# Reordering the down products of both feed-forwards and moving x1's division by its rms behind W_in's products

## The chip, the cores and the metric

The kernel runs on one core of a Trainium2 chip. The metric is device time in microseconds (us) of one execution; lower is better. TensorE (PE) does the matmuls, VectorE (DVE), ScalarE (ACT) and GpSimd (POOL) the elementwise work, SyncE (SP) issues most DMAs. Matmul results land in PSUM, everything else on the chip lies in SBUF.

## The reference

One layer of a streaming encoder in fp32, 1024 tokens of width 1024:

```
x1  = x  + 1/2 * SwiGLU_1(RMSNorm(x))          # 1024 -> 2*2816 -> 2816 -> 1024
h   = RMSNorm(x1)                              # x1 / rms(x1) * g_mix
q_A,k_A,v_A,q_B,k_B,v_B,gate_A,gate_B = h @ W_in
y   = sigmoid(gate_A)*(A(q_A,k_A,v_A) @ W_upA) + sigmoid(gate_B)*(B(q_B,k_B,v_B) @ W_upB)
x2  = x1 + y @ W_out
x3  = x2 + 1/2 * SwiGLU_2(RMSNorm(x2))
out = RMSNorm(x3)
```

A is chunked attention, B differential attention; both normalize q and k by head (an rms over 64 columns) before use. v and the gates are used as they come from W_in.

## The kernel before, in words

Every fp32 matmul is made of three: each operand is split into a rounded high part (a cast on ACT) and the remainder (a subtraction on DVE), and high*high, high*low and low*high are summed in PSUM (`mm3`, recorded at line 90). The split of a weight is lines 211 (ACT) and 215 (DVE), that of a stored hidden activation lines 785 (ACT) and 788 (DVE), that of the last hidden tiles 770 and 771, that of a transposed operand 448 (ACT) and 449 (DVE, reading PSUM).

**Down projection.** The 22 blocks of 128 hidden channels fall into two groups that are multiplied in the manner of Strassen and Winograd (`paired`: two groups of five pairs of blocks) and two plain blocks (`down`). A group has seven products, in the order of the tuple `PRODUCTS`. A product runs over five pairs and four row blocks c, 60 matmuls of 128x512, into four PSUM banks. `down_operand` makes the weight sums that products 3 to 6 need, on POOL (lines 352 to 358: T for products 5, 6 and 4, b12 for product 3). `quarter_sums` takes each of the four banks out of PSUM into the quarters c11, c12, c21, c22 of x or into the shared sums u2, a5, a7 (line 830). In the second group, `end`, the shared sums are added to the quarters on POOL: c22 += a5 after product 5; a5 += u2, c12 += a5 and a7 += u2 after product 6; c21 += a7 and c22 += a7, eight additions of 128x512, are kept in `later` and issued by `down` for its tiles t = 0 to 3. `residual` adds the saved first half of x to c11 on POOL in the first group.

**`down`** does for each row tile t of 128 rows and each half of 512 columns the two plain blocks: 6 matmuls into one bank, and line 916 on DVE adds it to x. Then it calls `done`, which is `after1` in the first feed-forward and `after2` in the second.

**`after1`** stores x1, norms it (`Norm`: Square with a running sum on ACT at line 475, the root on POOL at lines 455 and 456, x * 1/rms * gain on DVE at line 482), and `transpose_into_xT` turns the normed tile by eight PE transposes and splits it into xTh and xTl, the operand of W_in. **`after2`** norms x3 in the same way and stores the output.

**W_in** follows: for each group of 512 columns and each row tile 24 matmuls into a bank. q and k tiles are squared (ACT, 1136), summed by head (DVE, 1139), rooted (POOL, 455 and 456), scaled (DVE, 1145) and turned. v is split by 1196 (ACT) and 1197 (DVE), a gate copied by 1207 (ACT).

**What sets the order.** The program is written in the order of PE's work. Other work hangs on `pe.chain(keys, (delay, function), ...)`: a function is issued once PE's stream has gone on by that many ns, and `pe.settle(key)` issues what is still open on a key. So each engine's queue has a fixed order, and an instruction that waits holds up all behind it on its engine.

```
pe.chain((), (1000, store), (1300, norm.scale), (1600, lambda: norm.into_xT(t)))   # after1
pe.chain((), (1000, norm.stats), (2000, norm.scale), (1300, store))                # after2
```

Of the kernel before, what the change touches and what calls it, by code (L numbers as in the profile page):

```python
# [21 lines left out]
P = 128  # L22
# [29 lines left out]
assert PLAIN + 2 * sum(GROUPS) == NF  # L52
PRODUCTS = (1, 2, 5, 6, 4, 3, 7)

# [200 lines left out]
def kernel(ctx, tc, io, out):  # L255
# [17 lines left out]
    lam = cp.tile([P, 2], F32, name="lam")  # L273
    nlam = cp.tile([P, 1], F32, name="nlam")


# [49 lines left out]
    def ffn_weights(w_gu, w_down):  # L326
# [16 lines left out]
        def down_operand(p, top, bottom, ts, i):  # L343

            def piece():
                (b11, b12), (b21, b22) = [(w[:, :512], w[:, 512:]) for w in (weights.raw[top], weights.raw[bottom or top])]
                engine = nc.gpsimd
                if p == 5:  # L350
                    ts[i] = pools["T"][:, i] if i < 4 else pe.tile(pools["ffn"], [P, 512], F32, "sg", 3)
                    engine.tensor_tensor(ts[i], b12, b11, op=ALU.subtract)
                elif p == 6:
                    engine.tensor_tensor(ts[i], b22, ts[i], op=ALU.subtract)
                elif p == 4:
                    engine.tensor_tensor(ts[i], b21, ts[i], op=ALU.subtract)
                elif p == 3:
                    engine.tensor_tensor(b12, b22, b12, op=ALU.subtract)
                return {1: b11, 2: b21, 3: b22, 7: b12}.get(p, ts.get(i))

            if p == 1:
                return lambda: weights.raw[top][:, :512], top, [], 0
            return piece, top if p == 5 else bottom, {3: [bottom], 7: [top]}.get(p, []), p in (3, 4, 5, 6)

# [132 lines left out]
    def ffn(pool, base, x_d, begin, when, after, gain, beside):  # L497
# [234 lines left out]
        class Hidden:  # L732
# [27 lines left out]
            def load_last(self):  # L760

                while len(self.rooms) >= 2 and self.n_last < PLAIN:
                    f = self.n_last
                    raw = last_raw(f)
                    h, l = last[f] = [
                        pool.tile([P, S], F32R, name="hl", tag=self.rooms.popleft()) for _ in range(2)
                    ]
                    pe.chain(
# [3 lines left out]
                    )  # L772
                    self.n_last += 1

            def next(self):
# [29 lines left out]

        hidden, last, hs = Hidden(), {}, {}

# [14 lines left out]
        def quarter_sums(n, p, c, ps):  # L822
# [12 lines left out]
            if p == 1:  # L835
                now = [copy(u2, ps)] if first else [plus(c11, ps), plus(u2, ps)]
            elif p == 2:
                now = [plus(c11, ps, u2) if first else plus(c11, ps)]
            elif p == 6:
# [10 lines left out]
            elif end and p == 6:  # L850
                pe.chain(
                    (x[c], ("acc", c)), (900, plus(a5, u2, engine=nc.gpsimd)),
                    (LATE, plus(c12, a5, engine=nc.gpsimd)), (LATE, plus(a7, u2, engine=nc.gpsimd)),
                )
            elif end and p == 7:
                later[c] = (x[4 + c], ("acc", c)), (0, plus(c21, a7, engine=nc.gpsimd)), (LATE, plus(c22, a7, engine=nc.gpsimd))

        later = {}

        def paired():  # L860
# [10 lines left out]
            for n, g in enumerate(GROUPS):  # L871
                for p in PRODUCTS:
# [16 lines left out]
                    if n == 0 and p in (2, 5):  # L889
                        for t in range(4, NT) if p == 2 else range(4):  # L890
                            cols = slice(0 if t >= 4 else 512, D)
                            nc.sync.dma_start(x[t][:, cols], x_d[t * P : (t + 1) * P, cols])
                    if n == 0 and p in (4, 3, 7) or (n, p) == (1, 1):
                        residual((4, 3, 7, 1).index(p))
                    if (n, p) == (1, 3):
                        gain()
            nth = first + -(-j // 2)

        def down(fs, done):

            first = nth
            for t in range(NT):
                ts = slice(t * P, (t + 1) * P)
                for c in range(2):
# [13 lines left out]
                    pe.chain((ps, x[t]), (610, add))  # L918
                if t < 4:
                    pe.chain(*later[t])  # L920
                elif t == 4:
                    for c in range(4):
# [69 lines left out]
    def after1(t, xt):  # L992

        if t == 0:
            new_xT(0)
        elif t == 4:
            new_xT(1)
        norm = Norm(fp, xt, gm[0])

        def store():  # L1000
            pe.settle(xt)
            nc.sync.dma_start(x1_d[t * P : (t + 1) * P, :], xt)
            norm.stats()

        pe.chain((), (1000, store), (1300, norm.scale), (1600, lambda: norm.into_xT(t)))

# [81 lines left out]
    def project_all(cols, evac):  # L1088

        for col in cols:  # L1090
            first = base_in + 4 * (col // 512)
            for t in range(NT):
                ps = banks["fill"]() if "fill2" not in banks or t % 2 == 0 else banks["fill2"]()
                pe.settle(("xT", t))
                for k in range(NK):
# [32 lines left out]
    def qk_evac(n, t, ps):  # L1128
# [6 lines left out]
        def square():  # L1135
            nc.scalar.square(qn, ps)

# [3 lines left out]
        def root():  # L1141
            box["r"] = rstd_of(ap, ss, HD, 8, "rs8")

        def normed():
# [44 lines left out]
    def v_evac(n, t, ps):  # L1189
# [5 lines left out]
            (ps, stg),  # L1195
            (95, lambda: nc.scalar.copy(sv[:, :, 0], ps3)),
            (600, lambda: nc.vector.tensor_tensor(sv[:, :, 1], ps3, sv[:, :, 0].bitcast(F32), op=ALU.subtract)),
            (1390, lambda: nc.sync.dma_start(v_d[n][t], stg.bitcast(F32))),
        )

    def g_evac(n, t, ps):
# [4 lines left out]
            (ps, gs),  # L1206
            (150, lambda: nc.scalar.copy(gs, ps)),
            (700, lambda: nc.sync.dma_start(g_d[t, :, i, c * 512 : (c + 1) * 512], gs)),
# [525 lines left out]
    def after2(t, xt):  # L1734
        norm = Norm(fp, xt, gf[0])

        def store():
            nc.sync.dma_start(out[t * P : (t + 1) * P, :], norm.y)

        pe.chain((), (1000, norm.stats), (2000, norm.scale), (1300, store))  # L1740

# [41 lines left out]
```

## Time and profile before

| | |
|---|---|
| median of 3 runs | 2212.17 us (2210.03 to 2213.1) |
| the profiled execution | 2211.59 us |
| its span, first to last instruction | 2209.5 us |
| mean granted TensorE clock | 0.990 |
| PE busy | 2139.8 us (97%) |
| DVE, ACT, POOL busy | 1449.5 (66%), 851.0 (39%), 846.1 (38%) us |

The span is cut into 40 slices of 55.2 us in the page's second part; each digit there is a busy share in tenths. Places are given in us from the span's start. The first feed-forward's paired products end and its plain ones begin at 644.95, the second's at 2165.76. In the timeline a row of several instructions gives their common time; a matmul's own time (0.39) is longer than the step from one to the next, since they are pipelined. A number in square brackets at the end of a row is the idle time before it, and what ended it.

### The profile page before, as it was taken

How to read it: one execution, taken by the hardware profiler on the slowest of the kernel's cores; microseconds unless marked ns; L12 is line 12 of the kernel's file. 1: busy time of each engine (PE TensorE's matmuls, PEld its weight loads, DVE VectorE, ACT ScalarE, POOL GpSimd, SP SyncE). 2: the span in 40 equal slices, each digit the busy share in tenths (PEclk: the TensorE clock that was granted, in tenths of full speed). 3: DMA queues.
4: the chain of work that ended last, by engine and by line, in shares of the span. 5: the costliest groups of instructions: out<-in, count | busy, mean ns of one | idle time of the engine just before them, and what ended most of it. 6: DMA issues, size and time to landing. Idle time of an engine off the chain costs nothing. (4 is left out here: it accounts for less than half of the span.)

```text
span 2209.5 us, 27922 instructions
## 1 busy us (share of the span) xinstructions
PE 2139.8 (97%) x10112; PEld 1783.0 (81%) x10112; DVE 1449.5 (66%) x2021; ACT 851.0 (39%) x1483; POOL 846.1 (38%) x749
## 2 busy tenths in 40 slices
PE   7999999999998998999999999999999999999996
PEld 6788888888876887888888887788788888888885
DVE  7768666687985435775665662534766666668895
ACT  5323323244333224665555552313332332334431
POOL 3645544352762313552111110000554545426483
PEclk9999999999999999999999999999999999999998
DMA  4234333376342445756544439523132332365431
GB/s 158 77 94 135 101 115 101 123 258 202 115 150 90 132 159 170 196 150 193 169 137 136 153 115 268 193 77 118 54 103 90 105 103 91 114 231 210 152 117 77
DMA packets 267602, 305.66 MB, mean 138 GB/s; under 512 B 17456, under 2 KB 177480, under 8 KB 267464
## 3 DMA queue, kind: packets, MB, share of 16 engines
q1 hardware_dynamic: 267320, 303.35, 43.1%
q8 instruction: 80, 1.31, 0.2%
q14 instruction: 58, 0.48, 0.1%
q0 software_dynamic: 144, 0.52, 0.1%
HBM read 210.21 MB, written 94.40 MB: 138 GB/s over the span
## 5 line engine op out<-in xcount | busy, mean ns | idle before, releaser
L211 ACT CAST wh<-w 128x1024 fp32r<-128x1024 f32 (+1 forms) x228 | 201.1, 900 | 400.7 <-PE mm L90 147.8
L90 PE MATMUL fill<-wh,xTh 128*128 128x512 f32 x824 | 328.1, 405 | 0.0
L90 PE MATMUL fill<-wh,xTl 128*128 128x512 f32 x816 | 315.2, 393 | 0.0
L215 DVE TENSOR_TENSOR wl<-w,wh 128x1024 fp32r<-128x1024 f32 (+1 forms) x227 | 286.7, 1278 | 35.3 <-ACT wh L211 34.8
L90 PE MATMUL fill<-wl,xTh 128*128 128x512 f32 x752 | 296.6, 394 | 0.0
L90 PE MATMUL mm<-xTl,wh 128*128 128x512 f32 (+1 forms) x572 | 220.7, 386 | 2.4 <-DVE xTl L614 1.8
L90 PE MATMUL mm<-xTh,wh 128*128 128x512 f32 (+1 forms) x572 | 221.6, 387 | 0.2 <-ACT xTh L448 0.2
L90 PE MATMUL mm<-xTh,wl 128*128 128x512 f32 (+1 forms) x572 | 220.2, 385 | 0.0
L90 PE MATMUL mm<-S,wh 128*128 128x512 f32 x640 | 197.0, 389 | 0.0
L90 PEld LDWEIGHTS fill<-wh,xTl 128*128 128x128 f32 x816 | 154.0, 189 | 33.1
L90 PEld LDWEIGHTS fill<-wh,xTh 128*128 128x128 f32 x824 | 155.7, 189 | 27.2
L90 PEld LDWEIGHTS fill<-wl,xTh 128*128 128x128 f32 x752 | 142.7, 190 | 23.3
L455 POOL TENSOR_SCALAR rs<-ss 128x1 f32<-128x1 f32 (+1 forms) x64 | 13.1, 205 | 337.2 <-ACT xn L475 237.6
L90 PEld LDWEIGHTS mm<-S,wh 128*128 128x128 f32 x640 | 120.1, 188 | 24.9
L215 DVE TENSOR_TENSOR wl<-tw,wh 128x1024 fp32r<-128x1024 f32 x80 | 124.9, 1562 | 9.3 <-ACT wh L211 9.3
L90 PEld LDWEIGHTS mm<-xTl,wh 128*128 128x128 f32 x572 | 108.6, 190 | 24.5 <-DVE xTl L614 2.2
L90 PE MATMUL mm<-wh,xTh 128*128 128x512 f32 x376 | 126.7, 390 | 0.0
L90 PEld LDWEIGHTS mm<-xTh,wh 128*128 128x128 f32 x572 | 108.6, 190 | 21.7 <-ACT xTh L448 0.7
L90 PEld LDWEIGHTS mm<-xTh,wl 128*128 128x128 f32 x572 | 108.4, 190 | 21.4 <-POOL wl L215 0.2
L90 PE MATMUL mm<-S,wl 128*128 128x512 f32 x320 | 124.5, 389 | 0.0
L90 PE MATMUL mm<-wh,xTl 128*128 128x512 f32 x360 | 121.3, 389 | 0.0
L335 POOL TENSOR_TENSOR tw<-w,w 128x512 f32<-128x512 f32 x40 | 55.0, 1376 | 152.2 <-DVE wl L215 103.7
(254 smaller groups left out, 4851.8 us busy)
## 6 DMA issues: line engine op xcount, KB each, us to landing
w<-in_w_ffn_gu SPq DMA_DIRECT2D x88, 512.0 KB, 4.3
raw<-hq_d SPq DMA_DIRECT2D x70, 512.0 KB, 3.7
hq_d<-xn SPq DMA_DIRECT2D x98, 256.0 KB, 4.5
w<-in_w_ffn_down SPq DMA_DIRECT2D x44, 512.0 KB, 5.6
w<-in_w_in SPq DMA_DIRECT2D x40, 512.0 KB, 4.3
hq_d<-x SPq DMA_DIRECT2D x42, 256.0 KB, 4.3
x_d<-x SPq DMA_DIRECT2D x16, 512.0 KB, 3.2
uq<-qa_d SPq DMA_DIRECT2D x32, 256.0 KB, 4.5
```

The lines of the kernel that those rows point to most:

```text
L90: self.nc.tensor.matmul(ps, lhs, rhs, **flags)
L211: self.nc.scalar.copy(h, w)
L215: (lo_engine or self.nc.vector).tensor_tensor(l, w, h.bitcast(F32), op=ALU.subtract)
L335: nc.gpsimd.tensor_tensor(t[:, :512], u0, g0, op=ALU.subtract)
L455: nc.gpsimd.tensor_scalar(r, ss, 1.0 / n, EPS, op0=ALU.mult, op1=ALU.add)
```

## The change

1. `PRODUCTS` becomes (1, 2, 5, 6, 7, 4, 3). Product 7 makes b12 itself; products 4 and 3 come last and take T and the raw b22. POOL's a7 += u2, c21 += a7 and c22 += a7 of the second group hang on product 7, so `later` goes. In the first group ACT copies both u2 and c11 out of product 1. The calls of `residual` and `gain` move.
2. `after1` has no norm any more. POOL multiplies x1 by the gain (line 1011 of the changed kernel, 128x1024), into the place of hidden tiles that are no longer used; ACT's Square sums into a column of `ss_x1`; after the last tile POOL makes all eight `r_x1` = 1/rms. The product x1 * gain is turned, and W_in's results are multiplied by `r_x1` where they leave PSUM: in the scale of ACT's Square for q and k with one POOL multiplication more on the head roots (line 1160), in ACT's copies for v and gates, and in DVE's subtraction for v. The transposes are due 4300 ns of PE's stream behind the store rather than 1600 behind the scale.
3. `after2` takes its normed tile from four such places, and the scale is due 2600 ns behind the statistics rather than 2000.

```diff
-PRODUCTS = (1, 2, 5, 6, 4, 3, 7)
+PRODUCTS = (1, 2, 5, 6, 7, 4, 3)
...
-                elif p == 3:
+                elif p == 7:
                     engine.tensor_tensor(b12, b22, b12, op=ALU.subtract)
                 return {1: b11, 2: b21, 3: b22, 7: b12}.get(p, ts.get(i))
...
-            return piece, top if p == 5 else bottom, {3: [bottom], 7: [top]}.get(p, []), p in (3, 4, 5, 6)
+            return piece, top if p == 5 else bottom, {3: [bottom], 7: [top]}.get(p, []), p in (4, 5, 6, 7)
...
             if p == 1:
-                now = [copy(u2, ps)] if first else [plus(c11, ps), plus(u2, ps)]
+                now = [copy(u2, ps), copy(c11, ps)] if first else [plus(u2, ps), plus(c11, ps)]
             elif p == 2:
-                now = [plus(c11, ps, u2) if first else plus(c11, ps)]
+                now = [plus(c11, ps)]
...
-                    (LATE, plus(c12, a5, engine=nc.gpsimd)), (LATE, plus(a7, u2, engine=nc.gpsimd)),
+                    (LATE, plus(c12, a5, engine=nc.gpsimd)),
                 )
             elif end and p == 7:
-                later[c] = (x[4 + c], ("acc", c)), (0, plus(c21, a7, engine=nc.gpsimd)), (LATE, plus(c22, a7, engine=nc.gpsimd))
-
-        later = {}
+                pe.chain(
+                    (x[4 + c], ("acc", c)), (900, plus(a7, u2, engine=nc.gpsimd)),
+                    (LATE, plus(c21, a7, engine=nc.gpsimd)), (LATE, plus(c22, a7, engine=nc.gpsimd)),
+                )
...
-                    if n == 0 and p in (4, 3, 7) or (n, p) == (1, 1):
-                        residual((4, 3, 7, 1).index(p))
-                    if (n, p) == (1, 3):
+                    if n == 0 and p in (6, 7, 4, 3):
+                        residual((6, 7, 4, 3).index(p))
+                    if (n, p) == (1, 4):
                         gain()
...
-                if t < 4:
-                    pe.chain(*later[t])
-                elif t == 4:
+                if t == 0:
                     for c in range(4):
                         pe.settle(("acc", c))
...
-        norm = Norm(fp, xt, gm[0])
-
-        def store():
+        box = {}
+
+        def spare(n):
+            return fp.tile([P, D], F32, name="xn", tag=pools["spare"][n])
+
+        def gained():
             pe.settle(xt)
             nc.sync.dma_start(x1_d[t * P : (t + 1) * P, :], xt)
-            norm.stats()
-
-        pe.chain((), (1000, store), (1300, norm.scale), (1600, lambda: norm.into_xT(t)))
+            box["y"] = spare(t % 3)
+            nc.gpsimd.tensor_tensor(box["y"], xt, gm[0], op=ALU.mult)
+            nc.scalar.activation(spare(3), xt, AF.Square, accum_out=ss_x1[:, t : t + 1])
+            if t == NT - 1:
+                nc.gpsimd.tensor_scalar(r_x1, ss_x1, 1.0 / D, EPS, op0=ALU.mult, op1=ALU.add)
+                nc.gpsimd.tensor_tensor(r_x1, r_x1, mhalf, op=ALU.pow)
+
+        def into_xT():
+            for kk in range(2):
+                transpose_into_xT(box["y"][:, kk * 512 : (kk + 1) * 512], t, 4 * kk)
+
+        pe.chain((("into", t),), (1000, gained), (4300, into_xT))
...
-            nc.scalar.square(qn, ps)
+            nc.scalar.activation(qn, ps, AF.Square, scale=r_x1[:, t : t + 1])
...
             box["r"] = rstd_of(ap, ss, HD, 8, "rs8")
+            nc.gpsimd.tensor_scalar(box["r"], box["r"], r_x1[:, t : t + 1], 1.0, op0=ALU.mult, op1=ALU.mult)
...
+        def stats():
+            norm.place = fp.tile([P, D], F32, name="xn", tag=pools["spare"][t % 4])
+            norm.stats()
...
-        pe.chain((), (1000, norm.stats), (2000, norm.scale), (1300, store))
+        pe.chain((), (1000, stats), (2600, norm.scale), (1300, store))
```

**Where instructions stand: POOL, the last products of the first feed-forward.** Before, from the last T of product 4 (the place of `sg`) to the first roots of x1; x is a quarter of the result, acc a shared sum, w a weight block whose second half becomes b12:

```order
L356 TENSOR_TENSOR sg<-w_4175,sg 128x512
L830 TENSOR_TENSOR x<-x,acc 128x512 x4
...
L830 TENSOR_TENSOR acc<-acc 128x512 x4
L358 TENSOR_TENSOR w_4061<-w_4175,w_4061 128x512
L830 TENSOR_TENSOR x<-x,acc 128x512 x4
L830 TENSOR_TENSOR acc<-acc 128x512 x4
L830 TENSOR_TENSOR x<-x,acc 128x512
L455 TENSOR_SCALAR rs<-ss 128x1
L456 TENSOR_TENSOR rs<-rs,mhalf 128x1
L830 TENSOR_TENSOR x<-x,acc 128x512 x2
```

And in the changed kernel (834 is line 830 before, 360 line 358, 358 line 356):

```order
L360 TENSOR_TENSOR w_3985<-w_4184,w_3985 128x512
L358 TENSOR_TENSOR T<-w_3987,T 128x512
L358 TENSOR_TENSOR T<-w_4026,T 128x512
L834 TENSOR_TENSOR acc<-acc 128x512 x4
L358 TENSOR_TENSOR T<-w_4135,T 128x512
L358 TENSOR_TENSOR T<-w_4137,T 128x512
L834 TENSOR_TENSOR x<-x,acc 128x512 x4
L358 TENSOR_TENSOR sg<-w_4184,sg 128x512
L834 TENSOR_TENSOR acc<-acc 128x512 x4
L834 TENSOR_TENSOR x<-x,acc 128x512 x8
L1011 TENSOR_TENSOR xn<-x,gain 128x1024 x8
L1014 TENSOR_SCALAR r_x_79<-ss_x_78 128x8
```

The eight additions into c21 and c22, which stood between the roots of the first tiles, now stand in one piece ahead of all tiles' work, and no root stands among the tiles.

**DVE, the plain products of the first feed-forward.** Before:

```order
L215 TENSOR_TENSOR wl<-w_4966,wh 128x1024
L916 TENSOR_TENSOR x<-mm,x 128x512 x3
L482 SCALAR_TENSOR_TENSOR xn<-x,rs,gain 128x1024
L916 TENSOR_TENSOR x<-mm,x 128x512 x2
L482 SCALAR_TENSOR_TENSOR xn<-x,rs,gain 128x1024
L449 TENSOR_TENSOR xTl<-t,xTh 128x4x128
L916 TENSOR_TENSOR x<-mm,x 128x512
L449 TENSOR_TENSOR xTl<-t,xTh 128x4x128
```

Changed (921 is line 916 before, 451 line 449, 792 line 788; the rows ahead of them too):

```order
L792 TENSOR_TENSOR xTh<-raw,xTh 128x1024
L215 TENSOR_TENSOR wl<-w_4735,wh 128x1024
L215 TENSOR_TENSOR wl<-w_4737,wh 128x1024
L834 TENSOR_TENSOR x<-x,mm 128x512 x4
L215 TENSOR_TENSOR wl<-w_4925,wh 128x1024
L215 TENSOR_TENSOR wl<-w_4950,wh 128x1024
...
L215 TENSOR_TENSOR wl<-w_4980,wh 128x1024
L921 TENSOR_TENSOR x<-mm,x 128x512 x6
L451 TENSOR_TENSOR xTl<-t,xTh 128x4x128
L921 TENSOR_TENSOR x<-mm,x 128x512
L451 TENSOR_TENSOR xTl<-t,xTh 128x4x128
```

No operation that waits for POOL's root stands between DVE's additions any more.

**DVE, the plain products of the second feed-forward.** Before:

```order
L916 TENSOR_TENSOR x<-mm,x 128x512 x3
L482 SCALAR_TENSOR_TENSOR xn<-x,rs,gain 128x1024
L916 TENSOR_TENSOR x<-mm,x 128x512 x2
L482 SCALAR_TENSOR_TENSOR xn<-x,rs,gain 128x1024
L916 TENSOR_TENSOR x<-mm,x 128x512 x2
```

Changed (484 is line 482 before):

```order
L921 TENSOR_TENSOR x<-mm,x 128x512 x4
L484 SCALAR_TENSOR_TENSOR xn<-x,rs,gain 128x1024
L921 TENSOR_TENSOR x<-mm,x 128x512 x2
L484 SCALAR_TENSOR_TENSOR xn<-x,rs,gain 128x1024
L921 TENSOR_TENSOR x<-mm,x 128x512 x2
```

The scale of tile t stood between the two additions of tile t + 1; now it stands behind both.

## Rows read from the trace of the kernel before

**Rows 1.** The page: busy us of each engine, share of the span, instructions.

```profile
PE 2139.8 (97%) x10112; PEld 1783.0 (81%) x10112; DVE 1449.5 (66%) x2021; ACT 851.0 (39%) x1483; POOL 846.1 (38%) x749
```

**Rows 2.** Busy time of each engine in four stretches; columns as in the first line.

```profile
core 0: us, PE busy (x) PEld busy (x) DVE busy (x) ACT busy (x) POOL busy (x), PEclk, DMA share, GB/s
600.00:640.00 40.00, 40.00 (x179) 33.10 (x178) 40.00 (x33) 15.45 (x19) 29.47 (x17) 1.00 0.42 131
644.95:704.92 59.97, 48.43 (x212) 38.24 (x211) 39.60 (x47) 21.23 (x37) 18.72 (x26) 0.89 0.31 112
2120.00:2160.00 40.00, 40.00 (x178) 33.14 (x177) 40.00 (x33) 13.34 (x17) 30.31 (x17) 1.00 0.32 106
2165.76:2209.50 43.74, 24.45 (x97) 18.68 (x95) 25.17 (x26) 9.21 (x16) 17.93 (x24) 0.86 0.24 97
```

**Rows 3.** PE's timeline, 644 to 700: start, time, engine, line, operation, [idle <-releaser].

```profile
644.95 0.39 PE L90 MATMUL mm<-wh,hl 128*128 128x512 f32 x1
...
651.98 0.39 PE L90 MATMUL mm<-wl,hl 128*128 128x512 f32 x1
...
658.86 1.11 PE L95 MATMUL t<-ident,xn 128*128 128x128 f32 x4 [2.73 <-DVE xTl L449]
...
660.89 0.78 PE L90 MATMUL mm<-wl,hl 128*128 128x512 f32 x1
...
665.17 0.62 PE L90 MATMUL mm<-wh,hl 128*128 128x512 f32 x2
...
666.32 1.03 PE L95 MATMUL t<-ident,xn 128*128 128x128 f32 x8
667.11 0.47 PE L90 MATMUL mm<-wl,hl 128*128 128x512 f32 x1
```

**Rows 4.** Waits of PE, 640 to 712: total us, times, longest.

```profile
PE t L95 <- DVE xTl L449: 10.7, 7, 2.7
```

**Rows 5.** DVE's timeline, 648 to 687.

```profile
655.93 2.27 DVE L482 SCALAR_TENSOR_TENSOR xn<-x,rs,gain 128x1024 f32<-128x1024 f32 x1 [1.60 <-ACT xTh L448]
```

**Rows 6.** PE's timeline, 2184 to 2196.

```profile
2184.65 0.50 PE L90 MATMUL mm<-wh,hl 128*128 128x512 f32 x1 [2.00 <-DVE x L916]
```

**Rows 7.** DVE's timeline, 2186 to 2205.

```profile
2186.73 2.30 DVE L482 SCALAR_TENSOR_TENSOR xn<-x,rs,gain 128x1024 f32<-128x1024 f32 x1 [1.53 <-POOL rs L456]
...
2201.15 0.68 DVE L916 TENSOR_TENSOR x<-mm,x 128x512 f32<-128x512 f32 x1
2204.01 1.29 DVE L482 SCALAR_TENSOR_TENSOR xn<-x,rs,gain 128x1024 f32<-128x1024 f32 x1 [2.18 <-POOL rs L456]
```

**Rows 8.** POOL's timeline, 616 to 651.

```profile
623.80 7.50 POOL L830 TENSOR_TENSOR acc<-acc 128x512 f32<-128x512 f32 x4
643.95 1.30 POOL L830 TENSOR_TENSOR x<-x,acc 128x512 f32<-128x512 f32 x1 [12.65 <-DVE acc L830]
```

**Rows 9.** DVE's timeline, 618 to 637.

```profile
618.67 2.32 DVE L788 TENSOR_TENSOR xTh<-raw,xTh 128x1024 fp32r<-128x1024 f32 x1
620.91 3.48 DVE L215 TENSOR_TENSOR wl<-w,wh 128x512 fp32r<-128x512 f32 x2
...
634.65 1.21 DVE L788 TENSOR_TENSOR xTh<-raw,xTh 128x1024 fp32r<-128x1024 f32 x1
635.78 2.35 DVE L215 TENSOR_TENSOR wl<-w,wh 128x1024 fp32r<-128x1024 f32 x2
```

**Rows 10.** Groups by line and shape, whole span: count | busy, mean ns | idle before.

```profile
L215 POOL TENSOR_TENSOR wl<-w,wh 128x1024 fp32r<-128x1024 f32 x1 | 2.4, 2359 | 0.1
L830 POOL TENSOR_TENSOR x<-x,acc 128x512 f32<-128x512 f32 x32 | 52.9, 1677 | 31.2 <-DVE acc L830 31.2
L456 POOL TENSOR_TENSOR rs<-rs,mhalf 128x8 f32<-128x8 f32 x32 | 52.6, 1645 | 2.7
L455 POOL TENSOR_SCALAR rs<-ss 128x8 f32<-128x8 f32 x32 | 6.3, 198 | 90.1 <-DVE ss L1139 87.8 <-DVE m L1325 2.2
L1145 DVE TENSOR_TENSOR qn<-fill,rs 128x512 f32<-128x512 f32 x32 | 22.0, 689 | 16.8 <-POOL rs L456 16.8
```

More of the change, by code (lines that the diff above doesn't have):

```diff
@@ L274 @@
     nlam = cp.tile([P, 1], F32, name="nlam")
+    ss_x1 = cp.tile([P, NT], F32, name="ss_x1")
+    r_x1 = cp.tile([P, NT], F32, name="r_x1")
     x1_d = dp.tile([S, D], F32, name="x1_d")
@@ L764, in load_last @@
                     raw = last_raw(f)
-                    h, l = last[f] = [
-                        pool.tile([P, S], F32R, name="hl", tag=self.rooms.popleft()) for _ in range(2)
-                    ]
+                    tags = [self.rooms.popleft() for _ in range(2)]
+                    used.update(tags)
+                    h, l = last[f] = [pool.tile([P, S], F32R, name="hl", tag=tag) for tag in tags]
                     pe.chain(
@@ L773, in load_last @@
                     self.n_last += 1
+                    if self.n_last == PLAIN:
+                        pools["spare"] = [f"e{i}" for i in range(8) if f"e{i}" not in used]
             def next(self):
@@ L804, in done @@
                 pe.later(self.at - pe.now, self.next)
-        hidden, last, hs = Hidden(), {}, {}
+        hidden, last, hs, used = Hidden(), {}, {}, set()
         def last_raw(f):
@@ L1093, in project_all @@
                 ps = banks["fill"]() if "fill2" not in banks or t % 2 == 0 else banks["fill2"]()
+                pe.settle(("into", t))
                 pe.settle(("xT", t))
@@ L1195, in v_evac @@
             (ps, stg),
-            (95, lambda: nc.scalar.copy(sv[:, :, 0], ps3)),
-            (600, lambda: nc.vector.tensor_tensor(sv[:, :, 1], ps3, sv[:, :, 0].bitcast(F32), op=ALU.subtract)),
+            (95, lambda: nc.scalar.activation(sv[:, :, 0], ps3, AF.Copy, scale=r_x1[:, t : t + 1])),
+            (600, lambda: nc.vector.scalar_tensor_tensor(
+                sv[:, :, 1], ps3, r_x1[:, t : t + 1], sv[:, :, 0].bitcast(F32), op0=ALU.mult, op1=ALU.subtract
+            )),
             (1390, lambda: nc.sync.dma_start(v_d[n][t], stg.bitcast(F32))),
@@ L1206, in g_evac @@
             (ps, gs),
-            (150, lambda: nc.scalar.copy(gs, ps)),
+            (150, lambda: nc.scalar.activation(gs, ps, AF.Copy, scale=r_x1[:, t : t + 1])),
             (700, lambda: nc.sync.dma_start(g_d[t, :, i, c * 512 : (c + 1) * 512], gs)),
```

## Prediction

> **What bounds the kernel now.** I read the page first: PE is busy for 2139.8 of 2209.5 us [rows 1], so a gain has to come out of some 70 us of idle PE and out of stretches at the lower clock. Then the busy times by stretch, to see where that lies. While the last paired products run, PE is busy 40.00 of 40 us, and so is DVE; POOL is busy for 29.5 and 30.3 [rows 2]. There PE sets the pace and DVE has nothing to spare. In the two stretches that the change is about PE does not set it: 48.43 busy of 59.97 us at a mean clock of 0.89, and 24.45 of 43.74 at 0.86 [rows 2].
>
> What these two should take follows from PE's timeline. 31 steps of a down matmul take 651.98 - 644.95 = 7.03 us, 0.2268 each, and eight transposes 667.11 - 666.32 = 0.79 [rows 3]. The first stretch runs from the first plain product to the first transposes of a q tile and holds 212 instructions [rows 2], 64 of them transposes: 148 x 0.2268 + 8 x 0.79 = 39.9 us. **It loses 20.0.** PE's waits say to whom: 10.7 us for seven waits on xTl [rows 4]. The gap of 2.73 is one of them [rows 3]: DVE's scale at 655.93 had itself waited 1.60 and then took 2.27, and xTl stands behind it [rows 3, 5]. Behind that gap PE goes at the lower of its two levels (1.2 instead of 2.4 GHz): ten matmuls from 660.89 to 665.17 take 4.28 us instead of 2.27 [rows 3]. So a long gap costs about 2.0 us more than its length.
>
> The second stretch has 96 matmuls, 21.8 us; from the last addition's start to the end of the span are another 2209.50 - 2201.15 = 8.35 [rows 7]. 43.74 - 30.1: **it loses 13.6.** Here PE waits for DVE's addition (2.00 at 2184.65) [rows 6], for the scale of tile t, waiting for POOL's root (1.53) and then taking 2.30, stands between the two additions of tile t + 1 [rows 7].
>
> **The change part by part.**
>
> *x1's norm, FFN1's end.* The roots and the eight scales leave the path between down product and transposes; 20.0 us can go. In their place stands POOL's x1 * gain, 128x1024 per tile. One such POOL operation is in the trace, 2.36 us [rows 10]; two additions of 512 alone (1.30 each) give 2.6 [rows 8], two at the worst of before, beside DVE, 4.6 (twice the 2.3 us that DVE's own 1024 takes there as they alternate) [rows 9]. PE needs 12 x 0.2268 + 0.79 = 3.51 us per tile. I take 2.6, since DVE's work here reads PSUM except for some W_in splits: no wait. At 4.6 it would be 8 x 1.1 = 8.8 us. r_x1 costs 0.20 + 1.65 [rows 10] once: with the last addition (0.68) and x1 * gain it is there 5.1 us behind the last plain product; the first W_in bank is full 7.0 us behind. Its cover is W_in's first 24 matmuls (5.4 us) and the last two tiles' transposes (1.6); were that gone, the 2 us would show.
>
> *Product order.* No matmul is added. Eight additions (c21, c22) move from the plain products, where they cost the DVE scale a microsecond each time (2.30 beside them, 1.29 alone [rows 7]), to product 7's end, that is into the stretch in which POOL idled for 12.65 us [rows 8]. At 1.68 mean [rows 10] they fill it (13.4 us). But DVE then no longer runs alone there. Beside POOL a 1024 split takes a step of 620.91 - 618.67 = 2.24 us, alone 635.78 - 634.65 = 1.13; a 512 one beside POOL 1.74 [rows 9]. Eight additions can thus hold DVE back by 8 x 1.1 = 8.8 us in each feed-forward; the low end is 0, if they fall on DVE's PSUM readers (0.68 as ever [rows 7]). DVE has no idle to take that from [rows 2], only its lead on PE: the split of the last-but-one hidden tile ends at 635.9 [rows 9], and PE reads it one fifth of a product ahead of the last fifth, 644.95 - 2 x 2.72 = 639.5, a lead of 3.6 us. I laid out DVE's and POOL's changed order from 617.7 on with these steps. In FFN1 three things come late: a weight split of product 3 by 0.9, the hidden tile of its fourth pair (behind more splits in the new order) by 4.3, and, behind the splits of W_in and the four quarters of product 3, the first addition of the plain products, for which PE's fifth bank waits 3.5: 8.7 us. In FFN2, without W_in's splits, 0.9 + 0.4 + 2.9 = 4.2. Three of these gaps are long ones, 3 x 2.0 at the lower clock: 6.0. In all 18.9; bounds 0 and 2 x 8.8 + 3.3 for three W_in splits beside x1 * gain + 8.0 for four long gaps = 28.9.
>
> In the rows the two engines seem to take turns. The Trainium skill (SBUF — State Buffer, section "SBUF: two separate sides") states that a DVE operation with two SBUF inputs and a GpSimd one exclude each other for the whole instruction, which speaks against putting more POOL work here. By that rule each of the 16 additions would cost its own 1.3 us, not 1.1, an estimate of 3 us more in the sum; the trace agrees to within 0.2, with 2.24 against 1.13 + 1.30.
>
> *ACT instead of DVE* for eight first-group sums: ACT is busy 15.45 of 40 us [rows 2]; nothing. *Earlier residuals*: POOL's additions sit ahead of T sums that are due a product later; nothing, at worst one product's slip.
>
> *The scale in FFN2* behind both additions: DVE needs 2 x 0.64 + 1.29 = 2.6 us per tile, PE 2.72, so PE paces it and the 13.6 can go.
>
> *W_in's evictions.* 32 POOL multiplications of 128x8, 0.20 each [rows 10] with a gap of 0.1, lengthen the q and k chains. DVE waits 16.8 us in all for that root [rows 10], but PE takes these tiles up groups later. I take 0.5; bounds 0 and 32 x 0.3 = 9.6. A scale in ACT's copies: no further instruction.
>
> **Sum**, against the profiled execution: 2211.6 - 20.0 - 13.6 + 8.7 + 4.2 + 6.0 + 0.5 = 2197.4. That execution lies 0.6 below the median, so **2198.0**.
>
> **The rivals.**
>
> *No new lag* (0.19). DVE's lead and the PSUM readers swallow the eight additions. Then 33.6 - 0.5 is gained, less a little: 2179 to 2188. For it: PE stays at 40.00 of 40 [rows 2] although POOL's additions already run beside DVE until 631.3. Against: DVE's 40.00.
>
> *FFN1's gain is given back in W_in* (0.10): earlier W_in matmuls wait for the weights' transfers or DVE's splits. Against it is the DMA share of 0.31 [rows 2]. Then only 5 to 7 us of FFN2 stay: 2205 to 2209.
>
> *POOL becomes the bound* (0.21), slower. The eight additions, then eight x1 * gain, stand in one queue between product 7 and r_x1. If each alternates with a DVE split, that gives the upper ends: 28.9 for lag and clock, 8.8 for x1 * gain at 4.6, and 4.8 if half the q and k chains hold PE up: 42.5 against 33.6, some 2221. It decides at 33.6 us; below that the kernel is no slower. For it: 2.30 against 1.29, the same operation with and without POOL [rows 7]. Against it: the upper ends must meet all at once.
>
> *The change does not do what it says* can be left out: the changed order has no scale between the additions.
>
> **How the numbers follow.** My own forecast has 0.50, and by its bounds goes from 2188 to 2207. About 0.2% (4.4 us) is what a measurement of this kernel tells from no change. Faster: 0.50 + 0.19 + 0.08 of the second rival = 0.77. Same: 0.02 + 0.07 from the third = 0.09. Slower: 0.14. The range from 2179 to 2215 leaves out the slow end of the third rival and the tip of the first.
>
> **What would show it.** Right: PE's waits on xTl and on the plain products' additions nearly gone; FFN1's stretch near 50 us, FFN2's near 36; POOL busy through the last product without its 12.65 us of idle; DVE's splits there at 2.2 instead of 1.2; some new waits of PE on DVE's splits of hidden tiles or weights in the last two products. No such waits: the first rival. POOL's x1 * gain at over 3.5 us and transposes waiting for it: the third. Waits of W_in's matmuls for DMA: the second. The forecast is wrong if FFN1's stretch does not shrink, or if q and k make PE wait in attention A.

## The result, and the profile after

The changed kernel takes 2190.64 us (median of 4 runs, 2188.51 to 2192.98) against 2211.88 for the kernel before: ratio 0.990, 95% interval 0.9888 to 0.9912. That is 21.2 us gained where 14.2 were forecast; the time lies in the range and in the forecast's own case. The profiled execution took 2190.83 us, its span is 20.4 us shorter.

The page of the changed kernel, its span and busy times [rows 1]:

```profile
span 2189.1 us, 27974 instructions
PE 2132.0 (97%) x10112; PEld 1777.7 (81%) x10112; DVE 1423.0 (65%) x2013; ACT 861.7 (39%) x1491; POOL 871.2 (40%) x775
```

PE has 7.8 us less to do with the same instructions (fewer at the lower clock), and 12.6 us less to wait. Busy times of the changed kernel in the two stretches that lost time before [rows 2], the first ending at the first transposes of q, the second at the last instruction. PEclk is the granted clock as a share of 2.4 GHz, so 0.50 is the lower level, 1.2 GHz:

```profile
core 0: us, PE busy (x) PEld busy (x) DVE busy (x) ACT busy (x) POOL busy (x), PEclk, DMA share, GB/s
648.20:693.91 45.71, 42.03 (x213) 33.77 (x212) 31.36 (x46) 22.85 (x38) 25.60 (x15) 1.00 0.51 180
2157.82:2189.10 31.28, 22.21 (x97) 17.76 (x95) 23.99 (x30) 9.21 (x16) 9.97 (x19) 0.92 0.33 135
```

The first went from 59.97 to 45.71 us with a clock of 1.00 instead of 0.89, the second from 43.74 to 31.28. What was paid for it stands ahead of the first stretch, which begins 3.25 us later, and inside it. PE's timeline of the changed kernel, the two gaps at the end of the first feed-forward:

```profile
643.08 0.73 PE L90 MATMUL fill<-wh,xTh 128*128 128x512 f32 x2 [2.92 <-DVE xTh L792]
...
656.32 0.50 PE L90 MATMUL mm<-wh,hl 128*128 128x512 f32 x1 [2.46 <-DVE x L921]
```

DVE's timeline of the changed kernel shows where these come from [rows 9]:

```profile
626.17 0.69 DVE L215 TENSOR_TENSOR wl<-sg,wh 128x512 fp32r<-128x512 f32 x1 [3.08 <-ACT wh L211]
626.78 0.69 DVE L215 TENSOR_TENSOR wl<-w,wh 128x512 fp32r<-128x512 f32 x1
...
631.70 9.12 DVE L215 TENSOR_TENSOR wl<-w,wh 128x512 fp32r<-128x512 f32 x5
640.74 2.28 DVE L792 TENSOR_TENSOR xTh<-raw,xTh 128x1024 fp32r<-128x1024 f32 x1
642.94 4.53 DVE L215 TENSOR_TENSOR wl<-w,wh 128x1024 fp32r<-128x1024 f32 x2
...
655.59 3.13 DVE L921 TENSOR_TENSOR x<-mm,x 128x512 f32<-128x512 f32 x5
```

and POOL's timeline beside it [rows 8]:

```profile
628.14 6.48 POOL L834 TENSOR_TENSOR acc<-acc 128x512 f32<-128x512 f32 x4 [2.66 <-DVE acc L834]
634.59 15.31 POOL L834 TENSOR_TENSOR x<-x,acc 128x512 f32<-128x512 f32 x8
657.00 7.09 POOL L1011 TENSOR_TENSOR xn<-x,gain 128x1024 f32<-128x1024 f32 x3 [7.10 <-DVE x L921]
665.85 2.39 POOL L1011 TENSOR_TENSOR xn<-x,gain 128x1024 f32<-128x1024 f32 x1 [1.76 <-DVE x L921]
```

POOL's idle 12.65 us are gone: the eight sums into c21 and c22 fill 634.59 to 649.90, behind those into a7. Five splits of 512 take 9.12 us beside POOL's sums, 1.82 each, where a split alone took a step of 0.61 (626.17 to 626.78); the hidden tile's split behind them ends at 643.02, and PE waits 2.92 us for it. x1 * gain takes 2.4 us and waits for DVE's addition, not the other way round.

In the second feed-forward the scale stands alone and behind both additions, and PE paces DVE. DVE's timeline of the changed kernel [rows 7]:

```profile
2172.50 0.69 DVE L921 TENSOR_TENSOR x<-mm,x 128x512 f32<-128x512 f32 x1 [0.24 <-PE mm L90]
2173.11 1.28 DVE L484 SCALAR_TENSOR_TENSOR xn<-x,rs,gain 128x1024 f32<-128x1024 f32 x1
2174.30 0.68 DVE L921 TENSOR_TENSOR x<-mm,x 128x512 f32<-128x512 f32 x1
```

### The profile page after: what moved, and what is told of

Same layout as the page of the kernel before. It is cut to its first block, busy times and chain, and to the rows that moved or that the text cites. A ratio compares the mean times of both kernels' runs of the same rounds, so it can differ in the third digit from the quotient of the medians.

```text
span 2189.1 us, 27974 instructions
## 1 busy us (share of the span) xinstructions
PE 2132.0 (97%) x10112; PEld 1777.7 (81%) x10112; DVE 1423.0 (65%) x2013; ACT 861.7 (39%) x1491; POOL 871.2 (40%) x775
## 4 chain that ended last, share of the span: by engine, by line
PE 57%; DVE 5%; POOL 2%; DMA 2%; issue 2%; SPq 1%; ACT 1%; POOLq 0%; DVEq 0%; ACTq 0%
PE fill L90 28%; PE mm L90 20%; PE t L95 3%; PE s L90 3%; PE t L90 2%; DVE wl L215 2%; PE o L90 2%; SPq L1632 1%; POOL x L834 1%; DVE xTh L792 1%; DVE x L834 1%; DMA uq<-qa_d 0%; DMA xn<-g_d 0%; DVE acc L834 0%; POOL S L598 0%
## 5 line engine op out<-in xcount | busy, mean ns | idle before, releaser
L215 DVE TENSOR_TENSOR wl<-w,wh 128x1024 fp32r<-128x1024 f32 (+1 forms) x227 | 293.7, 1308 | 37.2 <-ACT wh L211 36.5
L457 POOL TENSOR_SCALAR rs<-ss 128x8 f32<-128x8 f32 (+1 forms) x56 | 11.5, 206 | 290.3 <-ACT xn L477 204.6
L90 PEld LDWEIGHTS mm<-xTh,wl 128*128 128x128 f32 x572 | 108.3, 189 | 21.2 <-POOL wl L215 0.2
```

The source lines that it names most:

```text
L90: self.nc.tensor.matmul(ps, lhs, rhs, **flags)
L215: (lo_engine or self.nc.vector).tensor_tensor(l, w, h.bitcast(F32), op=ALU.subtract)
L457: nc.gpsimd.tensor_scalar(r, ss, 1.0 / n, EPS, op0=ALU.mult, op1=ALU.add)
```

## The experiments

Four stretches of each profiled execution, in us: from the start to the first plain down product of the first feed-forward, from there to the first transposes of q, from there to the first plain product of the second feed-forward, and to the end. They are differences of start times in PE's timeline.

| kernel | to plain 1 | to q | to plain 2 | to the end |
|---|---|---|---|---|
| before | 644.95 | 59.97 | 1460.84 | 43.74 |
| changed | 648.20 | 45.71 | 1463.91 | 31.28 |
| product order alone | 649.84 | 58.13 | 1462.75 | 40.78 |
| x1's division alone | 645.02 | 43.93 | 1461.10 | 43.65 |
| last scale alone | 644.94 | 57.11 | 1461.67 | 34.98 |
| changed, sums late | 644.93 | 46.47 | 1463.80 | 35.00 |
| changed, no q and k multiplications | 649.86 | 44.07 | 1462.93 | 31.24 |
| changed, c22 late in the first | 648.73 | 44.92 | 1457.92 | 31.23 |
| changed, x1 * gain on DVE | 649.71 | 49.15 | 1463.38 | 30.96 |
| order by feed-forward | 645.53 | 43.97 | 1463.33 | 31.17 |
| the same, no q and k multiplications | 645.30 | 44.45 | 1463.66 | 31.19 |
| changed, x1 * gain twice | 648.64 | 57.32 | 1463.33 | 31.21 |
| changed, one long gap | 649.64 | 51.89 | 1463.19 | 31.28 |

The third column is not moved by any edit in a way that could be told from its spread: 1457.92 to 1463.91, both ends with the same change in them. Where nothing of the stretch to q was edited (before, last scale alone) it still differs by 2.9 us, with the clock. So differences of 3 us in the second or third column of one execution are not read as an edit's by themselves. The last column is steadier: 30.96 to 31.28 in the eight kernels that have both the moved scale and the early sums there, 34.98 and 35.00 in the two that have the moved scale with late sums.

**The product order alone.** The changed kernel with both norms and W_in's results as before.

```diff
-PRODUCTS = (1, 2, 5, 6, 4, 3, 7)
+PRODUCTS = (1, 2, 5, 6, 7, 4, 3)
```

> The new product order with the early sums alone; both norms and W_in as before. My theory (the gain comes from the scales that no longer stand in DVE's way, the order alone pays its own lag): FFN1 keeps the two waits of 2.9 and 2.5 us in its last products and plain ones and wins some 4 us as DVE's scales run at 1.28 instead of 2.30; FFN2 wins some 4 us in the same way. About 2209 us, within 4 us of the kernel before. Rival (the early sums are what makes the plain stretches short): over half of the 21 us, 2201 or less.

Measured: 2211.21 us, ratio 0.9999 (0.9989 to 1.0008). The first column is 4.9 us longer, with the same 2.92 us wait and the lower clock behind it, the last 3.0 shorter. The first transposes of q come at 707.97, 3.1 us later than before, so the 4 us that I expected to win in the first feed-forward did not come; the 4 in the second came as 3. DVE's timeline of this kernel in the second feed-forward:

```profile
2182.02 1.28 DVE L484 SCALAR_TENSOR_TENSOR xn<-x,rs,gain 128x1024 f32<-128x1024 f32 x1 [1.53 <-POOL rs L458]
2183.22 1.28 DVE L921 TENSOR_TENSOR x<-mm,x 128x512 f32<-128x512 f32 x2
2186.03 1.28 DVE L484 SCALAR_TENSOR_TENSOR xn<-x,rs,gain 128x1024 f32<-128x1024 f32 x1 [1.53 <-POOL rs L458]
```

The scale is down to 1.28 from the first tile on, but the chain addition, root, scale, addition still takes 4.01 us per tile against PE's 2.72. Early sums shorten an operation in the chain; they do not take the chain apart. By themselves they give back what they win.

**x1's division alone.** The kernel before with the changed `after1` and the r_x1 at W_in's results.

```diff
-        pe.chain((), (1000, store), (1300, norm.scale), (1600, lambda: norm.into_xT(t)))
+        pe.chain((("into", t),), (1000, gained), (4300, into_xT))
```

> x1's division moved behind W_in's products, and nothing else; c21 and c22 get their sums between the x1 * gain of the first tiles. My theory: no waits in the last products (5.4 us less than in the changed kernel), but POOL has 2 x 1.3 + 2.4 = 5.0 us per tile for the first four against PE's 3.5, some 6 us of waits; the middle of the kernel is 3 us longer as in the changed kernel, because of the 32 POOL multiplications. FFN1's stretch of 60 us goes to about 51; about 2204 us. Rival (the sums must be out of the way first): FFN1's stretch stays over 56 us, 2210 us or more. Second rival (the 3 us in the middle come from elsewhere): the middle from the first q transposes to FFN2's plain products stays at 1460.8 us.

Measured: 2196.61 us, ratio 0.993 (0.9915 to 0.9945), 7 us better than expected. The first two columns together end at 688.95, before at 704.92 and in the changed kernel at 693.91. POOL's timeline of this kernel:

```profile
648.90 2.41 POOL L1012 TENSOR_TENSOR xn<-x,gain 128x1024 f32<-128x1024 f32 x1 [3.60 <-DVE x L920]
651.26 2.55 POOL L834 TENSOR_TENSOR x<-x,acc 128x512 f32<-128x512 f32 x2
653.77 2.40 POOL L1012 TENSOR_TENSOR xn<-x,gain 128x1024 f32<-128x1024 f32 x1
656.13 2.50 POOL L834 TENSOR_TENSOR x<-x,acc 128x512 f32<-128x512 f32 x2
```

and PE's timeline, the first transposes and the longer of its two waits for POOL:

```profile
653.64 1.04 PE L95 MATMUL t<-ident,xn 128*128 128x128 f32 x8
...
661.05 1.09 PE L95 MATMUL t<-ident,xn 128*128 128x128 f32 x8 [0.51 <-POOL xn L1012]
```

POOL has its 4.9 us per tile, as expected, but PE waits for it only 0.5 and 0.3 us. The transposes are now due 4300 ns of PE's stream behind the store, and PE goes on with plain products meanwhile: the first x1 * gain is done at 651.31, 2.3 us before PE turns it, and POOL loses that lead only by the third tile. The expected 6 us of waits were wrong. This later place of the transposes belongs to the edit; no run separates its share from that of the division. The third column is near that of before, though the 32 multiplications are in.

**The last scale alone.** The kernel before with the changed `after2`.

```diff
-        pe.chain((), (1000, norm.stats), (2000, norm.scale), (1300, store))
+        pe.chain((), (1000, stats), (2600, norm.scale), (1300, store))
```

> Only the last norm's scale moved behind both additions. My theory: DVE then needs 2 x 0.64 + 2.30 = 3.6 us for each of the first three or four tiles, while POOL adds c21 and c22 beside it, and 2.6 after, against PE's 2.72; some 3 us of the 13.6 stay. FFN2's end of 43.7 us goes to about 34; about 2202 us. Rival (early sums needed): 39 us or more, 2207 us or more.

Measured: 2201.98 us, ratio 0.9957 (0.9942 to 0.9972). The last column is 35.0. DVE's timeline of this kernel:

```profile
2173.94 2.31 DVE L482 SCALAR_TENSOR_TENSOR xn<-x,rs,gain 128x1024 f32<-128x1024 f32 x1 [0.90 <-POOL rs L456]
2176.17 1.27 DVE L918 TENSOR_TENSOR x<-mm,x 128x512 f32<-128x512 f32 x2
```

Beside POOL's late sums the scale takes 2.31. Time and last column came as expected. Taking the chain apart is worth 8.8 of the 12.5 us in the last column, the early sums the other 3.7.

**The changed kernel with late sums.** c21 and c22 get a7 in the plain stretch, as before; a7 itself is early.

```diff
-                    (LATE, plus(c21, a7, engine=nc.gpsimd)), (LATE, plus(c22, a7, engine=nc.gpsimd)),
                 )
+                later[c] = (x[4 + c], ("acc", c)), (0, plus(c21, a7, engine=nc.gpsimd)), (LATE, plus(c22, a7, engine=nc.gpsimd))
...
-                if t == 0:
+                if t < 4:
+                    pe.chain(*later[t])
+                elif t == 4:
```

> The changed kernel, but c21 and c22 get their shared sum in the plain stretch as before (a7 itself stays early). My theory: PE's waits of 2.9 and 2.5 in FFN1 and 0.6 in FFN2 go with the contention on DVE; some 6 us of waits for x1 * gain come in FFN1, 3 us in FFN2. About 2194 us, 1 to 5 us slower than the changed kernel. Rival (the lag is from the order of DVE's own work, not from POOL's eight sums): the waits of 2.9 and 2.5 stay, and it is 2199 us.

Measured: 2189.3 us, ratio 0.9896 (0.9879 to 0.9912), the same as the changed kernel. DVE's timeline, the rows that answer to those of the changed kernel:

```profile
631.67 5.86 DVE L215 TENSOR_TENSOR wl<-w,wh 128x512 fp32r<-128x512 f32 x5
638.20 1.23 DVE L792 TENSOR_TENSOR xTh<-raw,xTh 128x1024 fp32r<-128x1024 f32 x1 [0.67 <-ACT xTh L789]
```

DVE's order is the same; with POOL's sums into c21 and c22 gone from there (those into a7 stay) the five splits take 5.86 instead of 9.12 us, the hidden tile is there 3.6 us sooner, and the 2.92 us wait is gone. That shows the lag to be POOL's sums beside DVE's splits. In its place PE waits 3.7 us for x1 * gain (6 were expected), and the last column is 3.7 us longer. The first transposes of q come 2.5 us sooner than in the changed kernel, so the sums for the most part only move their price; the 1 to 5 us that I expected to lose did not show.

**The changed kernel without the multiplications in the q and k chains.**

```diff
-            nc.scalar.activation(qn, ps, AF.Square, scale=r_x1[:, t : t + 1])
+            nc.scalar.square(qn, ps)
...
-            box["r"] = rstd_of(ap, ss, HD, 8, "rs8")
-            nc.gpsimd.tensor_scalar(box["r"], box["r"], r_x1[:, t : t + 1], 1.0, op0=ALU.mult, op1=ALU.mult)
+            box["r"] = rstd_of(ap, ss, HD, 8, "rs8", e_x1[:, t : t + 1])
```

> The changed kernel without the 32 POOL multiplications: the head's sum of squares is taken of the unscaled q or k, and eps / r^2 (per token, one POOL operation of 128x8 more) takes the place of eps under the root; the result is the same. My theory (these multiplications, in the chain from W_in's bank to the stored q, are why attention A waits longer for q): PE's waits for the loaded q go from 10.6 us back to about 8.5, the time to about 2188 us. Rival (q is waited for longer because PE comes to attention A with less slack behind it, whatever the chain): they stay at 10 us or more, and the time at 2190 to 2191.

Measured: 2187.95 us, ratio 0.9892 (0.9875 to 0.9908), which overlaps the changed kernel's interval. PE's waits over the whole span speak for the rival: the wait for q, first in the changed kernel and then in this one, is what it was (8.5 us before).

```profile
PE s L90 <- DMA uq<-qa_d: 10.6, 2, 6.4
```

```profile
PE s L90 <- DMA uq<-qa_d: 10.4, 2, 6.5
```

So the median alone, which fits my theory, would have misled. This execution shows something else. PE's timeline, the same two gaps as in the changed kernel:

```profile
643.09 0.74 PE L90 MATMUL fill<-wh,xTh 128*128 128x512 f32 x2 [2.92 <-DVE xTh L793]
656.32 0.50 PE L90 MATMUL mm<-wh,hl 128*128 128x512 f32 x1 [0.86 <-DVE x L922]
```

and busy times from 643 to 648, first of this kernel, then of the changed one (columns as above):

```profile
643.00:648.00 5.00, 4.91 (x14) 3.88 (x15) 5.00 (x5) 1.04 (x1) 5.00 (x3) 0.66 0.42 147
```

```profile
643.00:648.00 5.00, 4.92 (x22) 4.05 (x22) 5.00 (x5) 1.05 (x1) 5.00 (x3) 1.00 0.49 152
```

Behind the same gap the clock fell here (0.66) and not there (1.00). PE is then 1.6 us later at the plain products, and its next wait, which ends with the same DVE addition, is 1.6 us shorter: 656.32 in both. The lower clock cost nothing.

**c22 late in the first feed-forward alone.**

```diff
-                    (LATE, plus(c21, a7, engine=nc.gpsimd)), (LATE, plus(c22, a7, engine=nc.gpsimd)),
+                    (LATE, plus(c21, a7, engine=nc.gpsimd)), *(() if after is after1 else [(LATE, plus(c22, a7, engine=nc.gpsimd))]),
                 )
+                later[c] = (x[4 + c], ("acc", c)), (0, plus(c22, a7, engine=nc.gpsimd))
```

> The changed kernel, but in the first feed-forward the four additions into c22 come in the plain stretch, one per tile, ahead of that tile's x1 * gain; c21 and a7 stay early. My theory (lag in proportion to POOL's work beside DVE's splits): the wait of 2.5 goes, that of 2.9 falls to 1 to 2.9, x1 * gain at 3.7 us per tile costs under 1 us: about 2188 us, POOL's sums done by about 644. Rival (all of the lag is made by a7 and c21, ahead): 2190 to 2191, both waits stay.

Measured: 2188.11 us, ratio 0.9894 (0.9879 to 0.9909): not to be told from the changed kernel. DVE's timeline:

```profile
632.21 9.12 DVE L215 TENSOR_TENSOR wl<-w,wh 128x512 fp32r<-128x512 f32 x5
...
643.46 3.44 DVE L215 TENSOR_TENSOR wl<-w,wh 128x1024 fp32r<-128x1024 f32 x2
```

The sums that remain still stand beside the five splits, so the wait of 2.95 stays; only the two later splits are faster (3.44 against 4.53). The second wait goes from 2.46 to 1.64; 0.35 of that is the addition, which starts sooner by as much, the rest is PE, which comes to the plain products about 0.5 us later in this execution. So the rival was right on the first wait, and my theory in part on the second: it matters which splits the sums meet.

**Each feed-forward with its own order.** Old order and late sums in the first, new order and early sums in the second.

```diff
+        old = after is after1
+        order = (1, 2, 5, 6, 4, 3, 7) if old else PRODUCTS
...
-                for p in PRODUCTS:
+                for p in order:
...
+            elif end and p == 7 and old:
+                later[c] = (x[4 + c], ("acc", c)), (0, plus(c21, a7, engine=nc.gpsimd)), (LATE, plus(c22, a7, engine=nc.gpsimd))
```

> Each feed-forward with the order that its end wants: products 1, 2, 5, 6, 4, 3, 7 and late sums in the first, 1, 2, 5, 6, 7, 4, 3 and early sums in the second; both norms as in the changed kernel. My theory (the early sums cost the first feed-forward 5 us, for DVE has W_in's splits beside them and no scale to spare, and win the second 3.7, as DVE's scale runs alone): first q transposes near 689, last stretch near 31 us, 2185 to 2186 us. Rival (the parts can't be added): as the changed kernel, 2190.

Measured: 2184.61 us, ratio 0.9879 (0.9864 to 0.9893), q transposes at 689.50, last column 31.17. The parts add up as expected, and this is the lowest median of the study, though its interval still touches the changed kernel's.

**x1 * gain on DVE.**

```diff
-            nc.gpsimd.tensor_tensor(box["y"], xt, gm[0], op=ALU.mult)
+            nc.vector.tensor_tensor(box["y"], xt, gm[0], op=ALU.mult)
```

> The changed kernel with x1 * gain on DVE (1.2 us alone) instead of POOL (2.4). My theory (POOL has room there, DVE has not: 4 x 0.64 + 1.2 = 3.8 us per tile against PE's 3.5): the transposes wait for DVE again, 2 to 4 us more, 2192 to 2195 us. Rival (POOL's 2.4 us or its queue is what still holds the transposes up): 2190 or less.

Measured: 2193.44 us, ratio 0.992 (0.9905 to 0.9935), as expected, though the interval touches the changed kernel's. The trace is clearer: the first transposes of q come at 698.86, 4.95 us later, and the waits on xTl are back, 9.9 us over the whole span against 4.9 in the changed kernel:

```profile
PE t L95 <- DVE xTl L451: 9.9, 9, 2.0
```

POOL, though half as fast at it (2.4 us against 1.22), is the better engine where DVE sets the pace of the tiles.

**Both better orders and no multiplications.** The orders by feed-forward and the kernel without the multiplications in one.

```diff
-            box["r"] = rstd_of(ap, ss, HD, 8, "rs8")
+            box["r"] = rstd_of(ap, ss, HD, 8, "rs8", e_x1[:, t : t + 1])
...
+        order = (1, 2, 5, 6, 4, 3, 7) if old else PRODUCTS
```

> The product order and sums of each feed-forward as its end wants them, and no POOL multiplication in the q and k chains (eps / r^2 under the root instead). My theory (PE does not wait for those multiplications, so taking them out gives nothing that can be measured): as with the mixed orders alone, 2183 to 2186 us, waits for the loaded q between 8 and 11 us. Rival (they cost 2 to 3 us, as the median of the run without them suggested): 2181 to 2183.

Measured: 2185.8 us, ratio 0.9876 (0.9856 to 0.9896); the wait for q is 9.3 us. One of the four executions took 6722.72 us, which nothing here explains; it is in the median (without it 2185.2) and not in the ratio. Again no gain from the multiplications' absence.

**x1 * gain done twice.** The line stands there a second time.

```diff
             nc.gpsimd.tensor_tensor(box["y"], xt, gm[0], op=ALU.mult)
+            nc.gpsimd.tensor_tensor(box["y"], xt, gm[0], op=ALU.mult)
```

> The changed kernel with each x1 * gain done twice on POOL, 4.8 us per tile instead of 2.4. My theory (POOL has 3.5 us per tile, PE's pace, so the change had 1.1 us per tile to spare): the transposes now wait for POOL by about 1.3 us at seven tiles, 9 to 12 us in all, 2200 to 2203 us. Rival (the later tiles' wait hides behind W_in's first tiles): under 4 us more.

Measured: 2202.32 us (one run), 11.7 more than the changed kernel. PE's waits over the whole span:

```profile
PE t L95 <- POOL xn L1012: 9.8, 8, 2.1
```

The price lies in the range worked out, though not all of it is waits for POOL. PE's timeline, the first of the eight waits, then busy times behind it (columns as above):

```profile
662.33 1.44 PE L95 MATMUL t<-ident,xn 128*128 128x128 f32 x8 [2.09 <-POOL xn L1012]
```

```profile
664.00:666.00 2.00, 2.00 (x6) 1.61 (x5) 0.82 (x2) 0.40 (x1) 1.92 (x2) 0.50 0.00 0
```

Behind this wait, which follows one of 2.47 us for the plain products' addition, the clock fell to 0.50; behind the other seven, 0.25 to 1.80 us long, it stayed at 1.00. So the rival in which POOL becomes the bound had the right mechanism. Its 4.6 us per tile did not occur in the changed kernel, where x1 * gain took 2.4: DVE has only two splits of weights in those tiles.

**One long gap.** x1 * gain of tile 4 done four times.

```diff
-            nc.gpsimd.tensor_tensor(box["y"], xt, gm[0], op=ALU.mult)
+            for _ in range(4 if t == 4 else 1):
+                nc.gpsimd.tensor_tensor(box["y"], xt, gm[0], op=ALU.mult)
```

> The changed kernel with x1 * gain of tile 4 alone done four times on POOL, 7.2 us more at one place. My theory (one gap, after which POOL catches up): a single wait of PE of 4 to 6 us for that tile's transposes. If a long gap always brings the lower clock, as the prediction's sum had it, the stretch behind it runs at 0.5 for some 4 us and the kernel is 7 to 8 us slower than the changed one; if it comes only sometimes, the clock may stay at 1.00 there and it is 4 to 6 us slower.

Measured: 2197.79 us (one run), 7.2 more. PE's timeline, then busy times from 680 on (columns as above):

```profile
679.37 1.97 PE L95 MATMUL t<-ident,xn 128*128 128x128 f32 x8 [4.81 <-POOL xn L1012]
```

```profile
680.00:684.00 4.00, 4.00 (x14) 3.43 (x13) 1.70 (x3) 2.08 (x3) 2.56 (x2) 0.50 0.04 17
684.00:688.00 4.00, 4.00 (x20) 3.28 (x20) 1.98 (x3) 2.26 (x5) 1.45 (x1) 0.83 0.28 114
```

Here the clock fell behind the gap, and here it cost, as no later wait took it up: the first transposes of q come 7.6 us later than in the changed kernel, 2.8 more than the gap.

## Why the prediction was right, and where its sum was off

The direction and the mechanism held: the two tails shrank, POOL's idle time filled up, DVE's splits slowed, and in the first feed-forward new waits on a hidden tile and on the plain products' addition came. The sum was off by some 6 us. With the lower clock put to the three longest gaps, its terms go to the columns of the table like this:

| column | forecast | measured |
|---|---|---|
| to plain 1 | 0.9 + 4.3 + 2.0 = +7.2 | +3.3 |
| to q | -20.0 + 3.5 + 2.0 = -14.5 | -14.3 |
| to plain 2 | 0.9 + 0.4 + 0.5 = +1.8 | +3.1 |
| to the end | -13.6 + 2.9 + 2.0 = -8.7 | -12.5 |

That the second column agrees is luck: some 3 us too much was put down there as gain (2.1 that were no loss, and 1.2 of short waits that stay), and some 3 too much as lag and lower clock. Term by term:

- *FFN1's 20.0 and FFN2's 13.6 lost us can go.* The stretches are 14.3 and 12.5 us shorter. Of the first's 20.0, 11.5 were waits (59.97 - 48.43) and 6.4 busy time that the changed kernel does not need (48.43 - 42.03), most of it from the lower clock; the last 2.1 were no loss, as PE is still busy for 42.03 us with all of it at 1.00, not for 39.9. The first steps behind transposes are longer, which the 39.9 leave out: in the changed kernel those at 666.45 take 0.98 and the matmul behind them 0.32, where 0.79 and 0.23 were reckoned. Besides the wait of 2.46, 1.2 us of shorter waits stay. x1's division alone takes 16.0 us from the way to q, the scale's place and the early sums 8.8 and 3.7 from the end.
- *Lag in FFN1: 0.9 + 4.3 ahead of the plain products, 3.5 in them.* Measured 0, 2.92 and 2.46, 5.4 instead of 8.7. The two larger waits came at the places named. The run with late sums shows the cause to be the one named.
- *Lag in FFN2: 0.9 + 0.4 + 2.9 = 4.2.* None of the three came; there is one wait of 0.59, for a split of the plain products' weights. This term was mis-sized. The changed kernel there, DVE's timeline, then PE's:

```profile
2144.56 3.48 DVE L215 TENSOR_TENSOR wl<-w,wh 128x512 fp32r<-128x512 f32 x2
2147.96 2.31 DVE L792 TENSOR_TENSOR xTh<-raw,xTh 128x1024 fp32r<-128x1024 f32 x1
...
2161.74 1.93 DVE L921 TENSOR_TENSOR x<-mm,x 128x512 f32<-128x512 f32 x3
```

```profile
2159.48 0.50 PE L90 MATMUL mm<-wl,hl 128*128 128x512 f32 x1 [0.59 <-DVE wl L215]
```

  Two splits of 512, not five, stand ahead of the hidden tile, and it comes in time. The first addition, to which 2.9 was put, is done by 2162.4, and PE takes up its fifth bank at 2164.1. DVE came to it 3.9 us after PE began the plain products, against 7.4 in the first feed-forward; which step of the layout made it later is not on record.
- *Lower clock behind three long gaps: 6.0.* This was the largest mis-sized term. There were two gaps, and in the changed kernel's profile the clock stayed at 1.00 behind both. The step took "a long gap costs 2.0 more" from one gap, in a stretch in which gap followed gap. Seven profiles have the gap of 2.92 to 2.95 at 643: in four the clock fell (0.66 from 643 to 648) and the next wait was 0.86 to 0.90 us, in three it did not (1.00) and the next wait was 1.64 to 2.47. The loss was taken up.
- *q and k chains: 0.5.* The prediction had named a wait of PE in attention A as a sign of being wrong. The two runs without these multiplications show no effect of them. The wait for the loaded q is 9.0 to 10.6 us in the kernels with x1's division moved and 8.0 to 8.5 in those without; what makes that difference is open. It is not these multiplications.

The rivals: *no new lag* (2179 to 2188) failed by the two waits. That *FFN1's gain is given back in W_in* did not happen: from W_in's first matmul to 800 us, shortly before attention A begins, PE has one wait, 0.5 us for xTl, and none for a DMA. *POOL becomes the bound* did not happen either, since its upper ends did not meet; doubling x1 * gain made it so.

By the trace, a split of 512 beside POOL's sums takes 1.82 us, alone 0.61, and a POOL addition alone 1.30 [rows 8]. The rule that I weighed (the Trainium skill, SBUF — State Buffer, section "SBUF: two separate sides") is that a DVE operation with two SBUF inputs and a GpSimd one that reads SBUF exclude each other for a whole instruction. By that rule it would be 0.61 + 1.30 = 1.91 here, an estimate with one addition to each split; the trace agrees with it to 0.09.

What the change as a whole hides is that one of its three parts is worth nothing by itself. The product order alone changes nothing (0.9999): 3.1 us lost up to q, 3.0 won at the end. Beside the other two parts it costs the first feed-forward 5.0 us (693.91 against 688.95) and wins the second 3.7, so it belongs to the second alone. The other two parts together, without it, were not run; their gains by themselves, 14.8 and 9.4 us, add up to 24.2 as an estimate, against 21.2 for the whole change.

## What to carry to other kernels

Where a chain crosses engines once per tile (add, square, root, scale, add), look first for what in it must not be there: a per-row factor commutes with a matmul and can be put where the result leaves PSUM. Work moved into an engine's idle time is free only if no operation of the neighbour that it slows is on the critical path just there, so the same move can be right at one end of a kernel and wrong at the other: test it at each place by itself. And a loss just ahead of another wait may be no loss at all; a sum that adds both counts it twice.

## What the runs showed of the hardware that I had not expected

Nearly the same gap of PE, 2.92 to 2.95 us at the same place of seven kernels, was followed by the lower clock in four profiles and not in three, and I found nothing in the traces that tells them apart (two of the three lie some 0.5 us later in the span, the third does not). Nor does the length alone decide elsewhere: a gap of 4.81 us was followed by it, and so was one of 2.09 (behind one of 2.47 that was not), but seven of 0.25 to 1.80 us within the next 36 us were not. A price for the lower clock read from one execution is therefore one draw of several.
